# RWKV keys of a hybrid decoder layer: four keys first, products within the chunks one head pair later

## Chip, cores and metric

One core of one Trainium2 chip runs the whole program. The metric is device time in microseconds (us): 2528.46 us before the change, the median of three runs (2526.56, 2528.46, 2529.1).

## What is computed

One decoder layer on a sequence of 2048 tokens with 1024 channels. The input is normalised and modulated, projected once to all branches (RWKV-7, Mamba-2, gated linear attention), the branches are gated, merged and projected out. What the change touches is the RWKV branch, cut here to its keys and its recurrence:

```python
w = w0 + tanh(wd) @ w_up
decay = exp(-exp(-softplus(-w) - 0.5))
a = sigmoid(a0 + ad @ a_up)
kk = heads(k * k_k)
kk = kk / maximum(sqrt(sum(kk * kk, axis=-1, keepdims=True)), 1e-12)
k = k * (1 + (a - 1) * k_a)
# per token, state 64x64 per head:
sa = state @ -kk_t
state = state * w_t + sa * (kk_t * a_t) + v_t * k_t
y_t = state @ r_t
```

There are 8 heads of 64 channels. "The length of a key" below is the root of the sum of squares by which `kk` is divided.

## The kernel before

The sequence is worked in four quarters of 512 tokens (T). In each quarter, `mamba_gla` does the other two branches, then `rwkv` does this one, then 18 projections of merge logits follow (`gates_ahead` at the point "end"). After the last quarter `phase_o` does merging and output for all quarters.

A projection (`proj`, L322 to L332) makes one tile of 128 channels by 512 tokens with 24 matmuls (three for each of 8 slices of the input channels, weights and input split into a high and a low part), into one of two PSUM banks named mm. The weights come by DMA in halves of a tile, 512 columns each, and are split by ScalarE (L346) and VectorE (L347); `Weights` keeps three halves ahead in an order that `m_weights` and `r_weights` list in advance.

`rwkv` (L800) projects wd and ad, puts them through tanh and a split (L803 to L805), and then calls `rw_keys` (L829) for each of the four head pairs (two heads of 64 channels on 128 partitions). `rw_keys` for a head pair:

- makes decay and iclr logits with six matmuls on 64 rows each, three to bank pA from partitions 0 to 63 and three to pB from partitions 64 to 127 (L839), and from them the running decay G and its inverse GI (L841 to L848) and ta (L853);
- projects one tile of merge logits (`gates_ahead` at "r0" to "r3"), the key k (L855) and the receptance r (L867), each key and receptance mixed with its predecessor token by `rw_mix` (L822 to L825);
- finds the key's lengths: square (L858), a matmul with a block of ones (L860, to pA), Relu, Ln, Exp on ScalarE (L861 to L863);
- forms ar and bk, two tiles of 512 by 2 columns (L865 to L877, VectorE);
- makes the products within the chunks: for each of 8 chunks of 64 tokens and each of two heads one matmul bk times ar (L887), 64 rows by 128 columns, head 0 to bank pA and head 1 to bank pB, four chunks at a time, so that one head pair takes two passes over the same two banks; VectorE masks each bank into A (L890, four instructions for a head pair).

After the four head pairs, `rw_inverse` inverts 32x32 blocks of A on VectorE after a trip through DRAM (at a lower priority, offset INV), `rw_values` projects values and gates, `rw_merge` and `rw_chain` run the recurrence over 8 chunks.

The order on each engine is set when the program is built, by a scheduler that starts the ready instruction of highest priority. Priority is the order in the source; `later` moves work back (INV, POST, LATE) and, with the negative offset SOON, forward (the reads of the mm banks). On the chip each engine takes its instructions in that fixed order. Tiles of SBUF and PSUM are named by a tag that has a number of buffers: d, G, GI, ta, kn, r, sq, p2, cA, cB have one, k and y two, A eight, the PSUM banks pA, pB, pC, pE one and pD two.

Of the kernel before, what the change touches and what calls it, by code (L numbers as in the profile page):

```python
# [9 lines left out]
AF = mybir.ActivationFunctionType  # L10
ALU = mybir.AluOpType
# [3 lines left out]
P = 128  # L15
SEQ = 2048
D = 1024
T = 512
# [4 lines left out]
NCH = T // CH  # L23
NU = 4
# [69 lines left out]
def sb(g, tag, shape, dt=F32):  # L94
    n, bufs = SBUF_TAGS[tag]
    size = 1
    for x in shape[1:]:
        size *= x
    assert size <= n, (tag, shape)
    t = g.sp.tile([P, n], dt, name=tag, tag=tag, bufs=bufs)[0:shape[0], 0:size]  # L100
    if len(shape) == 3:
        t = t.rearrange("p (a b) -> p a b", a=shape[1])
    elif len(shape) == 4:
        t = t.rearrange("p (a b c) -> p a b c", a=shape[1], b=shape[2])
    return t


def small(g, tag, shape, bufs=2):
    return g.sp.tile(list(shape), F32, name=tag, tag=tag, bufs=bufs)


def pt(g, tag, shape=(P, T)):
    t = g.pp.tile([P, T], F32, name=tag, tag=tag, bufs=PSUM_TAGS[tag])
    size = 1
    for x in shape[1:]:
        size *= x
    t = t[0:shape[0], 0:size]
    if len(shape) == 3:
        t = t.rearrange("p (a b) -> p a b", a=shape[1])
    elif len(shape) == 4:  # L120
        t = t.rearrange("p (a b c) -> p a b c", a=shape[1], b=shape[2])
    return t


@contextmanager
def later(g, n):

    with g.tc.high_priority(-n):
        yield
# [188 lines left out]
def wtile(g, key):  # L318
    return g.A["w_pair"] if key == "dtgk" else g.A["w_in"][TILES[key]]
# [25 lines left out]
def split2(g, src, hi, lo):  # L345
    g.nc.scalar.copy(hi, src)  # L346
    g.nc.vector.tensor_tensor(lo, src, hi, ALU.subtract)  # L347
# [59 lines left out]
def mproj(g, hT):  # L407
    ps = pt(g, "mm")
    proj(g, ps, hT)
    return ps  # L410
# [328 lines left out]
def gate_keys(g, q, point):  # L739
    n = AHEAD.get(point, 0)  # L740
    at = g.planned[q]
    g.planned[q] += n
    return [("lg", b * 8 + i) for b, i in GATES[at:at + n]]


def gates_ahead(g, m, q, point):

    nc = g.nc
    for _ in range(AHEAD.get(point, 0)):
        ps = mproj(g, m.hT)  # L750
        t = sb(g, "th", [P, T])
        with later(g, SOON):
            nc.scalar.activation(t, ps, AF.Tanh, scale=0.5)  # L753
        nc.sync.dma_start(g.gates_dram[q, g.gated[q]], t)
        g.gated[q] += 1
# [1 line left out]


def r_weights(g, q):
    keys = ["wdad"]  # L760
    for pts in ((("k", "k"), ("r", "r")), (("v", "v"), ("g", "rg"))):
        for hp in range(NU):
            for point, key in pts:
                keys += gate_keys(g, q, ("r", point + str(hp))) + [(key, hp)]
    keys += gate_keys(g, q, ("r", "end"))
    return [wtile(g, key) for key in keys]
# [33 lines left out]
def rwkv(g, m, q):  # L800
    nc = g.nc
    wm = rw_mix(g, m, 12, "ysq")
    nc.scalar.activation(wm[0:64], wm[0:64], AF.Tanh)  # L803
    m.wm = sb(g, "wm", [P, T], F32R), sb(g, "wn", [P, T], F32R)
    split2(g, wm, *m.wm)  # L805
    hps = [rw_keys(g, m, q, i, str(i)) for i in range(NU)]
    with later(g, INV):
        rw_inverse(g, m, q, hps)
    for i, h in enumerate(hps):
        rw_values(g, m, q, i, h, str(i))  # L810
    rw_merge(g, m, hps)
    rw_chain(g, m, q, hps)


def rw_mix(g, m, i, tag):

    nc = g.nc
    ps = mproj(g, m.hT)
    o = sb(g, tag, [P, T])
    mu = g.v("mu", i)  # L820
    with later(g, SOON):
        nc.scalar.activation(o, ps, AF.Copy, scale=m.mu1[:, i:i + 1])  # L822
        nc.vector.scalar_tensor_tensor(o[:, 1:T], ps[:, 0:T - 1], mu, o[:, 1:T], ALU.mult, ALU.add)
        nc.vector.scalar_tensor_tensor(o[:, 0:1], m.prev[:, i:i + 1], mu, o[:, 0:1], ALU.mult, ALU.add)
        nc.vector.tensor_copy(m.prev[:, i:i + 1], ps[:, T - 1:T])  # L825
    return o


def rw_keys(g, m, q, hp, at):  # L829

    nc = g.nc
    h = Ctx()
    cb = lambda t: t.rearrange("p (c t) -> p c t", c=NCH)
    col = lambda t: t[:, hp:hp + 1]

    pw, pa = pt(g, "pA"), pt(g, "pB")
    for n, (a, b) in enumerate(((0, 0), (0, 1), (1, 0))):
        for o, js in ((pw, slice(0, 64)), (pa, slice(64, 128))):
            nc.tensor.matmul(o, m.up[a][js, hp * P:(hp + 1) * P], m.wm[b][js], start=n == 0, stop=n == 2)  # L839
    cs = sb(g, "d", [P, T])  # L840
    nc.scalar.activation(cs, pw, AF.Tanh, scale=0.5, bias=col(m.w0h))  # L841
    nc.vector.tensor_scalar(cs, cs, 1.0, None, ALU.add)
    nc.vector.tensor_tensor_scan(cs, g.scan[0], cs, 0.0, ALU.mult, ALU.add)
    G = sb(g, "G", [P, NCH, CH + 1])
    nc.gpsimd.memset(G[:, :, 0:1], 1.0)
    nc.scalar.activation(G[:, :, 1:], cb(cs), AF.Exp, scale=-0.5 * RW_C)
    GI = sb(g, "GI", [P, T])
    nc.scalar.activation(GI, cs, AF.Exp, scale=0.5 * RW_C)  # L848
    h.gc = small(g, "gc", [P, NCH], 4)
    nc.vector.tensor_copy(h.gc, G[:, :, CH])  # L850

    ta = sb(g, "ta", [P, T])
    nc.scalar.activation(ta, pa, AF.Tanh, scale=0.5, bias=col(m.a0h))  # L853
    gates_ahead(g, m, q, ("r", "k" + at))
    k = rw_mix(g, m, 4 + hp, ("k", "k", "y", "y")[hp])  # L855

    sq = sb(g, "sq", [P, T])
    nc.scalar.activation(sq, k, AF.Square, scale=g.v("k_k", hp))  # L858
    pn = pt(g, "pA")
    nc.tensor.matmul(pn, g.c("bones", P), sq, start=True, stop=True)  # L860
    nc.scalar.activation(sq, pn, AF.Relu, bias=g.c("m24"))  # L861
    nc.scalar.activation(sq, sq, AF.Ln, scale=65536.0, bias=g.c("epskk"))
    nc.scalar.activation(sq, sq, AF.Exp, scale=-0.5, bias=g.c("expkk"))  # L863
    kn = sb(g, "kn", [P, T])
    nc.vector.scalar_tensor_tensor(kn, k, g.v("k_k", hp), sq, ALU.mult, ALU.mult)  # L865
    gates_ahead(g, m, q, ("r", "r" + at))
    r = rw_mix(g, m, hp, "r")  # L867
    h.ar = sb(g, "ar", [P, NCH, 2, CH])
    h.bk = sb(g, "bk", [P, NCH, 2, CH])
    nc.vector.tensor_tensor(h.ar[:, :, 1], cb(r), G[:, :, 1:], ALU.mult)  # L870
    nc.vector.tensor_tensor(h.ar[:, :, 0], cb(kn), G[:, :, 0:CH], ALU.mult)
    nc.vector.scalar_tensor_tensor(kn, ta, 1.0, kn, ALU.add, ALU.mult)
    nc.vector.scalar_tensor_tensor(h.bk[:, :, 0], cb(kn), -0.5, cb(GI), ALU.mult, ALU.mult)
    nc.vector.tensor_scalar(ta, ta, col(m.kah), col(m.kab), ALU.mult, ALU.add)
    nc.vector.tensor_tensor(k, k, ta, ALU.mult)
    nc.vector.tensor_tensor(h.bk[:, :, 1], cb(k), cb(GI), ALU.mult)  # L876
    nc.vector.scalar_tensor_tensor(k, r, col(m.rkh), k, ALU.mult, ALU.mult)  # L877
    h.rk = k

    h.A = [sb(g, "A", [P, NCH, P]) for _ in range(2)]  # L880
    for c4 in range(0, NCH, 4):
        p = [pt(g, tag, [P, 4, P]) for tag in ("pA", "pB")]
        for i in range(4):
            c = c4 + i
            for j in range(2):
                js = slice(64 * j, 64 * j + 64)
                nc.tensor.matmul(p[j][:, i], h.bk[js, c].rearrange("p x t -> p (x t)"),  # L887
                                 h.ar[js, c].rearrange("p x t -> p (x t)"), start=True, stop=True)
        for j in range(2):
            nc.vector.tensor_tensor(h.A[j][:, c4:c4 + 4], p[j],  # L890
                                    g.c("gmask", P)[:, None, :].to_broadcast([P, 4, P]), ALU.mult)
    return h


def rw_values(g, m, q, hp, h, at):

    nc = g.nc
    gates_ahead(g, m, q, ("r", "v" + at))
    h.v = rw_mix(g, m, 8 + hp, "v")
    pb = pt(g, "pA")  # L900
    nc.tensor.matmul(pb, g.c("bones", P), h.rk, start=True, stop=True)
    p2 = sb(g, "p2", [P, T])
    nc.vector.tensor_tensor(p2, pb, h.v, ALU.mult)
    gates_ahead(g, m, q, ("r", "g" + at))
    pg = mproj(g, m.hT)
    th = sb(g, "th", [P, T])
    nc.scalar.activation(th, pg, AF.Tanh, scale=0.5)
    sg = sb(g, "sgo", [P, T])
    nc.vector.scalar_tensor_tensor(sg, th, 1.0, pg, ALU.add, ALU.mult)
    nc.vector.scalar_tensor_tensor(p2, p2, m.lnb[:, hp:hp + 1], sg, ALU.add, ALU.mult)  # L910
    nc.sync.dma_start(m.sd[q * NU + hp, 0], sg)
    nc.sync.dma_start(m.sd[q * NU + hp, 1], p2)
# [381 lines left out]
```

## Time and profile before

| what | value |
|---|---|
| median of three runs | 2528.46 us |
| the profiled execution, its own time | 2527.74 us |
| its span in the profile | 2526.0 us |
| TensorE (PE) busy | 2439.9 us, 97% |
| VectorE (DVE) busy | 1629.8 us, 65% |
| ScalarE (ACT) busy | 1236.1 us, 49% |

Busy time counts each engine's own instructions; a matmul's end is modelled and overlaps its successor, so for TensorE the distance between starts tells more than the duration. "PEclk" is the clock granted to TensorE as a share of 2.4 GHz; 0.5 is 1.2 GHz. A wait is idle time of an engine, put down to the instruction that ended it.

### The profile page before, as it was taken

The numbers are of one execution on the slowest core, as the hardware profiler recorded it, in microseconds if no ns is written. First come the engines' busy times: TensorE is split into PE (matmuls) and PEld (weight loads), VectorE is DVE, ScalarE is ACT, GpSimd is POOL, SyncE is SP. The second block draws the span as 40 slices with busy tenths as digits, with TensorE's granted clock in tenths as the row PEclk, the third lists the DMA queues.
The fourth block names the chain that finished last, engine by engine and source line by source line (L and its number), as shares of the span: only waits on it lengthen the run. The fifth ranks groups of instructions, "written<-read, shape, count | busy, mean of one in ns | idle before, by whom it ended". The sixth has DMA issues, their size and how long they took to land.

```text
span 2526.0 us, 39561 instructions
## 1 busy us (share of the span) xinstructions
PE 2439.9 (97%) x14756; PEld 1905.2 (75%) x14756; DVE 1629.8 (65%) x3180; ACT 1236.1 (49%) x2073; POOL 22.0 (1%) x68
## 2 busy tenths in 40 slices
PE   6999999999999999999999999999999999999998
PEld 4777777777777777777777777777777778787876
DVE  7694666546945664559566645694666547778696
ACT  4465643555656435556564355565643544233333
POOL 0000000000000000000000000000000000000000
PEclk9999999999999999999999999999999999999999
DMA  8322344343322442533234434322346367476571
GB/s 284 124 95 92 98 129 135 102 156 114 100 92 86 121 149 92 168 113 101 92 95 127 142 105 152 113 96 97 97 133 191 100 209 244 163 237 208 200 254 59
DMA packets 256916, 345.19 MB, mean 137 GB/s; under 512 B 63394, under 2 KB 112690, under 8 KB 256724
## 3 DMA queue, kind: packets, MB, share of 16 engines
q1 hardware_dynamic: 256724, 342.67, 42.2%
q8 instruction: 116, 1.90, 0.3%
q14 instruction: 76, 0.62, 0.1%
HBM read 275.40 MB, written 67.18 MB: 136 GB/s over the span
## 4 chain that ended last, share of the span: by engine, by line
PE 72%; DVE 12%; ACT 9%; issue 4%; DMA 3%; SPq 0%; DVEq 0%; ACTq 0%
PE mm L331 13%; PE mm L332 13%; PE mm L330 13%; PE mm L1153 3%; PE mm L1154 3%; PE mm L1155 3%; DVE wl L347 2%; DVE iU L939 1%; DVE iX L937 1%; PE pA L887 1%; ACT wh L346 1%; DMA wr<-in_w_in 1%; ACT L863 1%; PE pD L589 1%; PE pC L1044 1%
## 5 line engine op out<-in xcount | busy, mean ns | idle before, releaser
L330 PE MATMUL mm<-hTh,wh 128*128 128x512 f32 x2080 | 837.4, 403 | 4.5 <-ACT wh L346 3.1
L332 PE MATMUL mm<-hTh,wl 128*128 128x512 f32 x2080 | 836.3, 402 | 1.0 <-DVE wl L347 1.0
L331 PE MATMUL mm<-hTl,wh 128*128 128x512 f32 x2080 | 832.7, 400 | 0.0
L346 ACT CAST wh<-wr 128x512 fp32r<-128x512 f32 (+1 forms) x676 | 413.8, 618 | 778.6 <-PE mm L331 514.4
L347 DVE TENSOR_TENSOR wl<-wr,wh 128x512 fp32r<-128x512 f32 x672 | 458.3, 688 | 406.8 <-ACT wh L346 363.8
L330 PEld LDWEIGHTS mm<-hTh,wh 128*128 128x128 f32 x2080 | 393.9, 189 | 98.2 <-issue 9.8
L331 PEld LDWEIGHTS mm<-hTl,wh 128*128 128x128 f32 x2080 | 393.8, 189 | 91.7 <-issue 10.6
L332 PEld LDWEIGHTS mm<-hTh,wl 128*128 128x128 f32 x2080 | 393.7, 189 | 89.4 <-issue 7.4
L1153 PE MATMUL mm<-hTh,wh 128*128 128x512 f32 x256 | 100.1, 391 | 6.6 <-DVE th L1207 5.2
L1155 PE MATMUL mm<-hTh,wl 128*128 128x512 f32 x256 | 99.7, 390 | 0.0
L1154 PE MATMUL mm<-hTl,wh 128*128 128x512 f32 x256 | 99.7, 389 | 0.0
L753 ACT ACTIVATE th<-mm 128x512 f32<-128x512 f32 x96 | 57.0, 594 | 15.9 <-DMA gatesd<-th 7.7
L1153 PEld LDWEIGHTS mm<-hTh,wh 128*128 128x128 f32 x256 | 48.0, 188 | 18.6 <-issue 7.2
L1155 PEld LDWEIGHTS mm<-hTh,wl 128*128 128x128 f32 x256 | 48.1, 188 | 10.1
L1154 PEld LDWEIGHTS mm<-hTl,wh 128*128 128x128 f32 x256 | 48.1, 188 | 10.0
L887 PE MATMUL pA<-ar,bk 64*128 64x128 f32 x256 | 40.5, 291 | 13.6 <-DVE bk L876 13.6
L887 PEld LDWEIGHTS pA<-ar,bk 64*128 64x128 f32 x256 | 32.0, 187 | 26.1 <-DVE bk L876 20.3
L1154 PE MATMUL mm<-A,wh 128*128 128x512 f32 x128 | 50.8, 396 | 0.0
L1155 PE MATMUL mm<-A,wl 128*128 128x512 f32 x128 | 50.7, 396 | 0.0
L1153 PE MATMUL mm<-A,wh 128*128 128x512 f32 x128 | 50.7, 396 | 0.0
L937 DVE TENSOR_TENSOR iX<-iU,iN 128x31 f32<-128x31 f32 (+15 forms) x124 | 42.4, 342 | 3.4
L939 DVE TENSOR_TENSOR iU<-iU,iX 128x31 f32<-128x31 f32 (+15 forms) x124 | 42.3, 341 | 3.0
(712 smaller groups left out, 3664.7 us busy)
## 6 DMA issues: line engine op xcount, KB each, us to landing
wr<-in_w_in SPq DMA_DIRECT2D x520, 256.0 KB
gatesd<-th SPq DMA_DIRECT2D x96, 256.0 KB
wr<-in_w_branch SPq DMA_DIRECT2D x96, 256.0 KB
wr<-in_w_out SPq DMA_DIRECT2D x56, 256.0 KB
k<-gatesd SPq DMA_DIRECT2D x48, 256.0 KB
A<-in_x SPq DMA_DIRECT2D x16, 512.0 KB
A<-in_ada_w SPq DMA_DIRECT2D x16, 512.0 KB
y<-acsd SPq DMA_DIRECT2D x32, 256.0 KB
```

What stands on the lines that cost most here:

```text
L330: nc.tensor.matmul(ps, a, hh[k], start=k == 0, stop=False)
L331: nc.tensor.matmul(ps, a, hl[k], start=False, stop=False)
L332: nc.tensor.matmul(ps, b, hh[k], start=False, stop=k == KD - 1)
L346: g.nc.scalar.copy(hi, src)
L347: g.nc.vector.tensor_tensor(lo, src, hi, ALU.subtract)
L753: nc.scalar.activation(t, ps, AF.Tanh, scale=0.5)
L887: nc.tensor.matmul(p[j][:, i], h.bk[js, c].rearrange("p x t -> p (x t)"), h.ar[js, c].rearrange("p x t -> p (x t)"), start=True, stop=True)
L937: nc.vector.tensor_tensor(x, U[:, 0:a, t:t + 1].to_broadcast([nl, a, b]), N[:, t:t + 1, t + 1:].to_broadcast([nl, a, b]), ALU.mult)
L939: nc.vector.tensor_tensor(U[:, 0:a, t + 1:], U[:, 0:a, t + 1:], x, ALU.add)
L1153: nc.tensor.matmul(pb, a, yh, start=k == 0, stop=False)
L1154: nc.tensor.matmul(pb, a, yl, start=False, stop=False)
L1155: nc.tensor.matmul(pb, l, yh, start=False, stop=k == 3)
```

## The change

All four keys of a quarter are projected first, in a new function `rw_norm_keys`, which also finds their lengths: squares and sums key by key, then Ln for all four and Exp for all four. `rw_keys` takes key and inverse length from it and no longer makes the products within the chunks. These are in a new function `rw_within`, called for a head pair after `rw_keys` of the next one; it uses four banks (pA, pB, pC, pE) at once, so that the two passes become one. The decay and iclr logits go to the two buffers of pD instead of pA and pB, the key sums to pD instead of pA. Inside `rw_keys` the receptance and its two uses move behind the work on the key. The weight list follows. The inverse lengths sit in sq, p2, cA and cB.

```diff
 def r_weights(g, q):
-    keys = ["wdad"]
-    for pts in ((("k", "k"), ("r", "r")), (("v", "v"), ("g", "rg"))):
+    keys = ["wdad"] + [("k", hp) for hp in range(NU)]
+    for pts in ((("r", "r"),), (("v", "v"), ("g", "rg"))):
...
-    hps = [rw_keys(g, m, q, i, str(i)) for i in range(NU)]
+    ks = rw_norm_keys(g, m)
+    hps = []
+    for i, k in enumerate(ks):
+        hps.append(rw_keys(g, m, q, i, k, str(i)))
+        if i:
+            rw_within(g, hps[i - 1])
+    rw_within(g, hps[-1])
...
+def rw_norm_keys(g, m):
+    nc = g.nc
+    ks = []
+    for hp in range(NU):
+        k = rw_mix(g, m, 4 + hp, ("k", "k", "y", "y")[hp])
+        sq = sb(g, ("sq", "p2", "cA", "cB")[hp], [P, T])
+        nc.scalar.activation(sq, k, AF.Square, scale=g.v("k_k", hp))
+        pn = pt(g, "pD")
+        nc.tensor.matmul(pn, g.c("bones", P), sq, start=True, stop=True)
+        nc.scalar.activation(sq, pn, AF.Relu, bias=g.c("m24"))
+        ks.append((k, sq))
+    for k, sq in ks:
+        nc.scalar.activation(sq, sq, AF.Ln, scale=65536.0, bias=g.c("epskk"))
+    for k, sq in ks:
+        nc.scalar.activation(sq, sq, AF.Exp, scale=-0.5, bias=g.c("expkk"))
+    return ks
...
-    pw, pa = pt(g, "pA"), pt(g, "pB")
+    pw, pa = pt(g, "pD"), pt(g, "pD")
...
-    gates_ahead(g, m, q, ("r", "k" + at))
-    k = rw_mix(g, m, 4 + hp, ("k", "k", "y", "y")[hp])
-
-    sq = sb(g, "sq", [P, T])
-    nc.scalar.activation(sq, k, AF.Square, scale=g.v("k_k", hp))
-    pn = pt(g, "pA")
-    nc.tensor.matmul(pn, g.c("bones", P), sq, start=True, stop=True)
-    nc.scalar.activation(sq, pn, AF.Relu, bias=g.c("m24"))
-    nc.scalar.activation(sq, sq, AF.Ln, scale=65536.0, bias=g.c("epskk"))
-    nc.scalar.activation(sq, sq, AF.Exp, scale=-0.5, bias=g.c("expkk"))
     kn = sb(g, "kn", [P, T])
-    nc.vector.scalar_tensor_tensor(kn, k, g.v("k_k", hp), sq, ALU.mult, ALU.mult)
-    gates_ahead(g, m, q, ("r", "r" + at))
-    r = rw_mix(g, m, hp, "r")
+    nc.vector.scalar_tensor_tensor(kn, k, g.v("k_k", hp), inv, ALU.mult, ALU.mult)
     h.ar = sb(g, "ar", [P, NCH, 2, CH])
     h.bk = sb(g, "bk", [P, NCH, 2, CH])
-    nc.vector.tensor_tensor(h.ar[:, :, 1], cb(r), G[:, :, 1:], ALU.mult)
     nc.vector.tensor_tensor(h.ar[:, :, 0], cb(kn), G[:, :, 0:CH], ALU.mult)
...
     nc.vector.tensor_tensor(h.bk[:, :, 1], cb(k), cb(GI), ALU.mult)
+    gates_ahead(g, m, q, ("r", "r" + at))
+    r = rw_mix(g, m, hp, "r")
+    nc.vector.tensor_tensor(h.ar[:, :, 1], cb(r), G[:, :, 1:], ALU.mult)
     nc.vector.scalar_tensor_tensor(k, r, col(m.rkh), k, ALU.mult, ALU.mult)
     h.rk = k
-
+    return h
+
+
+def rw_within(g, h):
+    nc = g.nc
     h.A = [sb(g, "A", [P, NCH, P]) for _ in range(2)]
-    for c4 in range(0, NCH, 4):
-        p = [pt(g, tag, [P, 4, P]) for tag in ("pA", "pB")]
-        for i in range(4):
-            c = c4 + i
-            for j in range(2):
-                js = slice(64 * j, 64 * j + 64)
-                nc.tensor.matmul(p[j][:, i], h.bk[js, c].rearrange("p x t -> p (x t)"),
-                                 h.ar[js, c].rearrange("p x t -> p (x t)"), start=True, stop=True)
+    p = [[pt(g, tag, [P, 4, P]) for tag in tags] for tags in (("pA", "pB"), ("pC", "pE"))]
+    for c in range(NCH):
         for j in range(2):
-            nc.vector.tensor_tensor(h.A[j][:, c4:c4 + 4], p[j],
+            js = slice(64 * j, 64 * j + 64)
+            nc.tensor.matmul(p[c // 4][j][:, c % 4], h.bk[js, c].rearrange("p x t -> p (x t)"),
+                             h.ar[js, c].rearrange("p x t -> p (x t)"), start=True, stop=True)
+    for i in range(2):
+        for j in range(2):
+            nc.vector.tensor_tensor(h.A[j][:, 4 * i:4 * i + 4], p[i][j],
                                     g.c("gmask", P)[:, None, :].to_broadcast([P, 4, P]), ALU.mult)
-    return h
```

## Rows read from the trace of the kernel before

**Rows 1.** The page: its first line and part 1.

```profile
span 2526.0 us, 39561 instructions
...
PE 2439.9 (97%) x14756; PEld 1905.2 (75%) x14756; DVE 1629.8 (65%) x3180; ACT 1236.1 (49%) x2073; POOL 22.0 (1%) x68
```

**Rows 2.** Waits of PE, whole span: us in total, times, longest us.

```profile
PE pA L887 <- DVE bk L876: 13.6, 16, 1.2
...
PE pA L839 <- ACT wm L346: 6.5, 4, 1.6
...
PE pA L389 <- ACT r L391: 2.3, 3, 1.1
```

**Rows 3.** Timeline of PE, third head pair, first quarter: start, us, engine, line.

```profile
310.85 0.37 PE L887 MATMUL pA<-ar,bk 64*128 64x128 f32 x1 [0.88 <-DVE bk L876]
310.85 0.37 PE L887 MATMUL pB<-ar,bk 64*128 64x128 f32 x1
...
311.94 0.50 PE L330 MATMUL mm<-hTh,wh 128*128 128x512 f32 x1
...
312.83 0.82 PE L887 MATMUL pA<-ar,bk 64*128 64x128 f32 x5
...
314.46 0.50 PE L330 MATMUL mm<-hTh,wh 128*128 128x512 f32 x1
...
315.36 0.51 PE L839 MATMUL pA<-wm,up 64*128 64x512 f32 x1
...
316.59 0.50 PE L330 MATMUL mm<-hTh,wh 128*128 128x512 f32 x1
...
318.56 1.02 PE L860 MATMUL pA<-sq,cs 128*128 128x512 f32 x2
...
319.64 0.40 PE L330 MATMUL mm<-hTh,wh 128*128 128x512 f32 x1
...
321.01 0.39 PE L330 MATMUL mm<-hTh,wh 128*128 128x512 f32 x1
...
326.45 0.39 PE L330 MATMUL mm<-hTh,wh 128*128 128x512 f32 x1
```

**Rows 4.** Timeline of PE where the first quarter's keys begin.

```profile
260.34 0.39 PE L330 MATMUL mm<-hTh,wh 128*128 128x512 f32 x1
262.35 0.49 PE L839 MATMUL pA<-wm,up 64*128 64x512 f32 x1 [1.62 <-ACT wm L346]
262.35 0.49 PE L839 MATMUL pB<-wm,up 64*128 64x512 f32 x1
262.77 0.51 PE L331 MATMUL mm<-hTl,wh 128*128 128x512 f32 x1
```

**Rows 5.** Windows: PE, PEld, DVE, ACT, POOL busy (x), PEclk, DMA share, GB/s.

```profile
770.00:778.00 8.00, 8.00 (x20) 4.89 (x21) 5.60 (x10) 7.33 (x11) 0.00 (x0) 0.58 0.24 81
...
1774.00:1782.00 8.00, 8.00 (x20) 4.94 (x19) 5.43 (x10) 7.16 (x11) 0.00 (x0) 0.57 0.22 72
```

**Rows 6.** Groups of instructions, ACT, whole span: busy us, mean ns, idle before.

```profile
L862 ACT ACT_TABLE_LOAD x16 | 20.5, 1283 | 0.3
```

**Rows 7.** Window of one head pair, from products to products; columns as in rows 5.

```profile
310.80:333.60 22.80, 22.12 (x113) 17.11 (x113) 15.49 (x29) 12.81 (x19) 0.30 (x2) 1.00 0.43 122
```

**Rows 8.** Groups of DVE in that window: busy us, mean ns, idle before.

```profile
L347 DVE TENSOR_TENSOR wl<-wr,wh 128x512 fp32r<-128x512 f32 x7 | 4.8, 688 | 1.7 <-DMA gatesd<-th 1.4 <-ACT wh L346 0.2
L890 DVE TENSOR_TENSOR A<-pA,cs 128x512 f32<-128x512 f32 x2 | 1.4, 691 | 1.0 <-PE pA L887 1.0
...
L823 DVE SCALAR_TENSOR_TENSOR y<-mm,vec,y 128x511 f32<-128x511 f32 x1 | 0.7, 746 | 0.0
```

**Rows 9.** First quarter: the chain's last state steps, the merge logits' last reads (first, last start).

```profile
L1061 DVE TENSOR_TENSOR rs<-rs,gcu x7: 417/426/428, 457.5 to 501.3; 128x256 f32<-128x256 f32 x7
...
L753 ACT ACTIVATE th<-mm x18: 580/591/600, 404.4 to 560.7; 128x512 f32<-128x512 f32 x18
```

More of the change, by code (lines that the diff above doesn't have):

```diff
@@ L826, in rw_mix, with rw_keys @@
     return o
-def rw_keys(g, m, q, hp, at):
+def rw_norm_keys(g, m):
[14 more added lines that the diff above has]
+    return ks
+def rw_keys(g, m, q, hp, ks, at):
     nc = g.nc
     h = Ctx()
+    k, inv = ks
     cb = lambda t: t.rearrange("p (c t) -> p c t", c=NCH)
     col = lambda t: t[:, hp:hp + 1]
-    pw, pa = pt(g, "pA"), pt(g, "pB")
+    pw, pa = pt(g, "pD"), pt(g, "pD")
     for n, (a, b) in enumerate(((0, 0), (0, 1), (1, 0))):
```

## The prediction

> **What bounds the kernel now.** I read part 1 of the page first. TensorE (PE) is busy 2439.9 of 2526.0 us [rows 1], in a program whose projections follow each other without a gap, so a microsecond comes off the end only if PE works shorter or idles less. The second view is the list of PE's waits [rows 2]. The largest belongs to the part that is changed: all 16 groups of products within the chunks (L887, four head pairs in four quarters) wait for bk of their own head pair, 13.6 us in all. Another, 6.5 us in four waits, is that of the decay logits (L839) for the split of wd and ad at the start of each quarter's keys. The third view is PE's timeline, because idle time is not all that is lost there [rows 3]. The first 16 products of a head pair run two at a time on the two halves of the rows (two start at 310.85) and take 310.85 to 311.94, 1.09 us. The second 16 take 312.83 to 314.46, 1.63 us: five on pA go first and alone, because pB was planned to come free later.
>
> **Does PE time carry to the end?** In the first quarter the last step of the recurrence starts at 501.3 us, while the last projection of merge logits is read at 560.7 us [rows 9]. So 59 us of projections that depend on nothing in the branch still lie behind the chain. A saving among the keys moves both earlier, and the chain may even come some us later without PE running dry.
>
> **The change part by part.**
>
> 1. *Products one head pair later.* Products of pair i now stand behind the receptance of pair i+1; bk and ar of pair i are then complete. 12 of the 16 waits lose their cause. The fourth pair has no successor: its products follow the third's, and what fills the time is the projection of the first value, as now. I leave these four at the mean of 0.85 us (13.6/16). Gain 13.6 - 3.4 = 10.2 us; bounds 0 and 13.6.
>
> 2. *Four banks, one pass.* The second 16 products at the first's speed, without their lead-in: 0.88 instead of 1.63 us (1.09 less about 0.2 for the first pair; an estimate from rows 3), and one change between projection and product fewer, about 0.1 us (such a first matmul comes 0.33 instead of 0.23 us after its predecessor: an estimate from the same timeline). 0.85 x 16 = 13.6 us. Bounds: 0, if the order breaks the group up again, and 16 x 1.0.
>
> 3. *Start of a quarter's keys.* Now PE starts the first key at 260.34, then stands until 262.35 for wm [rows 4], because the logits come first in the order. Afterwards four keys, 4 x 24 matmuls at 0.227 us (5.44 us from 321.01 to 326.45 for 24 [rows 3]), stand ahead of the logits, 21.8 us in which wd and ad are long split. Gain 6.5 us [rows 2]; bounds 5 and 6.5.
>
> 4. *The clock behind that wait.* In the second and the fourth quarter, in the 8 us after that wait, PE was granted 0.58 and 0.57 of its clock [rows 5], that is, 1.2 GHz for most of the stretch; the engine had stood still just before. 8 x 0.42 + 8 x 0.43 = 6.8 us of PE's work lost. With nothing to wait for, I take all of it; bounds 0 (some other small stall does the same) and 6.8.
>
> 5. *Logits in pD.* The six matmuls of a later pair take 315.36 to 316.59, 1.23 us [rows 3], partly one by one because pB came free late. Two at once take 262.35 to 262.77, 0.42 us with the change to the next kind [rows 4]. Three such pairs: 0.42 + 2 x 0.23 = 0.88. Gain 0.35 x 12 = 4.2 us (the first pair of a quarter is mostly paired already); bounds 0 and 0.35 x 16 = 5.6. Their banks are read by two tanh, with nothing of VectorE in between.
>
> 6. *Table loads.* Ln and Exp each load a table for every key, 16 + 16 loads of 1.283 us (L862, and as many on L863) [rows 6]. Batched they are 8, and 31 us of ScalarE go. ScalarE is busy 49% [rows 1] and none of PE's waits that are left hangs on it, so I cost them at nothing; if the scheduler runs a Ln early because ScalarE is free, some loads come back, also for nothing. The key sums (L860) cost the same in pD: 318.56 to 319.64 less one matmul, 0.85 us.
>
> 7. *What is new.* Squares wait for p2 and cB, which the branch before uses last; k of pairs 2 and 3 waits for y to be written out; key sums share pD with the logits. No row shows these waits. Nearest is the wait of a matmul for a ScalarE read, up to 1.1 us (L389) [rows 2]. Bounds 0 and two such per quarter, 8.8; I take 1 us a quarter, 4 us. The SP queue issues as many DMAs as before, weights merely in another order; the DMAs of A for pairs 0 to 2 leave one pair later, but the inverse needs the fourth's too, and that comes where it came before. POOL's memset of G only follows the pair, as now.
>
> Sum: -10.2 - 13.6 - 6.5 - 6.8 - 4.2 + 4 = -37.3. The profiled execution took 2527.74 us (span 2526.0 plus 1.7 around it), 0.7 below the median. 2527.7 - 37.3 = 2490.4; set against the median, 2491 us.
>
> **VectorE, the nearest next bound.** Between two pairs PE now takes 22.80 us and VectorE is busy 15.49 of them, 68% [rows 7]. With keys gone from it, a pair's stretch on PE is 22.80 - 0.88 - 0.85 - 0.35 - 5.44 - 0.85 = 14.4 us. VectorE loses one mixing of k (0.75 at least) and about three weight splits (7 are in the window, 4 belong to the two projections that stay; 3 x 0.69) [rows 8]: 12.7 us, 88%. It fits, but with 1.7 us of air. The row behind: the four maskings of a pair take 4 x 0.69 = 2.8 us [rows 8], while 32 products in one pass would take about 2 us. The Trainium skill speaks against the change here: TensorEngine Tiling (Array Packing), section PSUM Bottleneck, warns that packing the array speeds up TensorE but not the emptying of PSUM, which may become the bottleneck. Worked as a mechanism of this kernel it is the second rival; by it the sum would be a loss, by the rows a gain; no row of before shows PSUM's emptying as what ends a stretch.
>
> **The rivals.**
>
> *A. Only the waits go.* The scheduler mixes products with projections, or frees banks unevenly, and neither products nor logits pack: parts 1, 3, 4 and 7 remain, -10.2 - 6.5 - 6.8 + 4 = -19.5, about 2509 us. For it: the scheduler did break up the second 16. Against: four banks that have been free for a whole pair give it no reason. Chance 0.13.
>
> *B. VectorE bounds the pairs (slower).* G, GI, d, ta and kn have one buffer each, so each pair's decay waits until the pair before has made ar, and VectorE also waits for ScalarE in that loop. If it stays filled no better than now, 12.7 / 0.68 = 18.7 us a pair, 4.3 more than PE's 14.4: 16 x 4.3 = 69 us against a gain of 37, about 2560 us. It turns the sign from 37.3 / 16 = 2.3 us more a pair, at a fill under 12.7 / 16.7 = 76%. Against: its present idle time is there because PE is slower, not because the loop is full. Chance 0.06.
>
> *C. Not later after all.* The scheduler's plan sets products as early as it thinks bk is ready; it has been about 0.9 us too early 16 times. If it pulls them ahead of the receptance in the same way, waits stay and passes stay broken: parts 3, 4, 5, 7, -6.5 - 6.8 - 4.2 + 4 = -13.5, about 2515 us. Against: the receptance has the higher priority and is always ready. Chance 0.07.
>
> *D. No difference.* New small waits and another half-clock stretch eat what is won. Chance 0.05.
>
> **How the numbers follow.** The forecast's own case has 0.69, and spans 2478 (all upper bounds and no new wait: -48.5, about 2480, and a little for the estimates) to 2502. 0.2% of the time, 5 us, is about what a measurement can tell from no change. Faster: forecast, A and C, 0.89; same: D, 0.05; slower: B, 0.06. The range takes in the forecast and A, with the estimates' error: 2476 to 2512.
>
> **What would show it.** In the changed kernel's waits, the products' line should show about four waits instead of 16, and the wait for wm should be gone; in PE's timeline, 32 products in about 2 us and six logits in under 0.9; the granted clock near 1.00 where the second and fourth quarters' keys begin; 8 loads, not 32, for Ln and Exp; from a quarter's first key to its last products about 9 us less. If VectorE is over 90% busy between pairs and PE waits for ar, bk or a mm bank, B is right and the forecast wrong.

## The result and the profile after

The changed kernel takes 2539.67 us (2533.62 to 2549.93), the one before beside it 2529.1 us (2526.56 to 2531.9): a ratio of 1.0053, 95% interval 1.0035 to 1.0071. (The ratios here are those on record; the quotient of the two medians is 1.0042.) It is slower by about half a per cent, where 2491 us and a gain were forecast. The profiled execution took 2540.58 us, with a span of 2538.8 us.

The page of the kernel after, its first line and part 1, answers to [rows 1]:

```profile
span 2538.8 us, 39623 instructions
...
PE 2438.0 (96%) x14756; PEld 1906.4 (75%) x14756; DVE 1628.5 (64%) x3180; ACT 1234.1 (49%) x2073; POOL 28.2 (1%) x68
```

ScalarE is as busy as before: the 31 us of table loads have not gone. Waits of PE after (us in total, times, longest us), for [rows 2]:

```profile
PE pD L844 <- ACT cA L842: 18.2, 4, 4.6
...
PE pE L354 <- ACT SV L346: 6.1, 5, 1.5
PE pA L907 <- DVE ar L892: 5.9, 4, 1.7
...
PE pD L844 <- ACT cB L842: 4.7, 4, 1.6
...
PE pD L844 <- ACT sq L842: 4.2, 4, 1.1
```

What was to go did go: four waits for products instead of 16, none for wm. In their place stand 12 waits of the key sums (L844) for ScalarE's squares, 18.2 + 4.7 + 4.2 = 27.1 us, and four waits of 1.46 us at the start of each quarter's keys for SV, a split of the branch before (L354). In the kernel before that line reads:

```profile
PE pE L354 <- ACT SV L346: 0.2, 1, 0.2
```

PE's timeline (start, us) for [rows 3]: the third key's sum, a later pair's products and logits, and the last pair's products:

```profile
285.30 0.39 PE L330 MATMUL mm<-hTh,wh 128*128 128x512 f32 x1
...
290.22 1.55 PE L844 MATMUL pD<-cA,cs 128*128 128x512 f32 x2 [4.54 <-ACT cA L842]
...
322.67 0.37 PE L907 MATMUL pA<-ar,bk 64*128 64x128 f32 x1
...
324.45 0.27 PE L907 MATMUL pE<-ar,bk 64*128 64x128 f32 x1
324.47 0.48 PE L865 MATMUL pD<-wm,up 64*128 64x512 f32 x2
...
336.47 0.37 PE L907 MATMUL pA<-ar,bk 64*128 64x128 f32 x1
...
353.75 1.13 PE L907 MATMUL pA<-ar,bk 64*128 64x128 f32 x8 [1.42 <-DVE ar L892]
354.81 0.50 PE L330 MATMUL mm<-hTh,wh 128*128 128x512 f32 x1
355.24 1.09 PE L907 MATMUL pB<-ar,bk 64*128 64x128 f32 x5
...
358.60 0.79 PE L331 MATMUL mm<-hTl,wh 128*128 128x512 f32 x1
```

The third sum waits 4.54 us. 32 products take one pass of 1.80 us (322.67 to 324.47), and a pair's stretch is 13.80 us long (to 336.47). The fourth pair's products follow directly behind the third's: they wait for ar, break up into eight on pA alone and a projection's matmul between, and end 4.85 us after they began (5.02, 5.18 and 3.46 us in the other quarters).

Four windows of the kernel after (columns as in rows 5): the keys of the first quarter, the half clock among them, one pair, the last pair's products.

```profile
265.60:305.00 39.40, 31.33 (x116) 21.78 (x115) 13.74 (x27) 34.09 (x46) 0.00 (x0) 0.96 0.21 74
290.80:294.20 3.40, 3.40 (x9) 2.31 (x8) 0.60 (x1) 2.36 (x3) 0.00 (x0) 0.50 0.21 77
322.70:336.50 13.80, 13.80 (x89) 11.20 (x88) 12.97 (x25) 5.76 (x11) 0.69 (x2) 1.00 0.43 118
355.60:362.40 6.80, 6.80 (x33) 5.80 (x32) 3.04 (x5) 0.00 (x0) 0.00 (x0) 0.50 0.39 82
```

Among the keys ScalarE is busy 34.09 of 39.4 us, 87%, and PE 80%. In the whole program they have 49% and 96%; in this stretch the order of the two is turned round.

### The profile page after: what moved, and what is told of

Same layout as the page of the kernel before. It is cut to its first block, busy times and chain, and to the rows that moved or that the text cites. A ratio compares the mean times of both kernels' runs of the same rounds, so it can differ in the third digit from the quotient of the medians.

```text
span 2538.8 us, 39623 instructions
## 1 busy us (share of the span) xinstructions
PE 2438.0 (96%) x14756; PEld 1906.4 (75%) x14756; DVE 1628.5 (64%) x3180; ACT 1234.1 (49%) x2073; POOL 28.2 (1%) x68
## 4 chain that ended last, share of the span: by engine, by line
PE 77%; ACT 9%; DVE 7%; DMA 3%; issue 3%; SPq 0%; ACTq 0%; DVEq 0%
PE mm L330 15%; PE mm L331 15%; PE mm L332 15%; PE mm L1173 3%; PE mm L1175 3%; PE mm L1174 3%; DVE wl L347 1%; ACT wh L346 1%; PE pC L1064 1%; PE pD L589 1%; PE pD L585 1%; DVE iU L959 1%; PE pE L1067 1%; PE pC L1047 1%; PE pD L844 1%
## 5 line engine op out<-in xcount | busy, mean ns | idle before, releaser
L521 DVE SCALAR_TENSOR_TENSOR ar<-G,cwh,ar 128x512 f32<-128x512 f32 x48 | 35.9, 749 | 3.9 <-ACT ar L517 3.3
L521 DVE SCALAR_TENSOR_TENSOR bk<-G,cwh,bk 128x512 f32<-128x512 f32 x48 | 35.7, 745 | 2.9 <-ACT bk L517 2.7
```

The lines of the kernel that those rows point to most:

```text
L521: nc.vector.scalar_tensor_tensor(o, R[:, j:j + T], m.cw[:, j * 8 + i:j * 8 + i + 1], o, ALU.mult, ALU.add)
```

## Where the time went: two theories

ScalarE's groups in the keys' stretch of the kernel after (busy us, mean ns, idle before): the loads ahead of Ln and of Exp.

```profile
L848 ACT ACT_TABLE_LOAD x4 | 5.1, 1283 | 0.1
L850 ACT ACT_TABLE_LOAD x3 | 3.8, 1283 | 0.1
```

ScalarE's timeline in the same stretch (start, us):

```profile
278.13 1.28 ACT L848 ACT_TABLE_LOAD   x1
279.42 0.72 ACT L848 ACTIVATE sq<-sq,cs 128x512 f32<-128x512 f32 x1
280.16 1.28 ACT L850 ACT_TABLE_LOAD   x1
281.46 0.72 ACT L850 ACTIVATE sq<-sq,cs 128x512 f32<-128x512 f32 x1
...
283.28 1.28 ACT L848 ACT_TABLE_LOAD   x1
...
285.32 1.28 ACT L850 ACT_TABLE_LOAD   x1
286.62 0.72 ACT L850 ACTIVATE p<-p,cs 128x512 f32<-128x512 f32 x1
...
287.75 0.68 ACT L828 ACTIVATE y<-mm,mu 128x512 f32<-128x512 f32 x1
...
289.45 0.72 ACT L842 ACTIVATE cA<-y,vec 128x512 f32<-128x512 f32 x1 [1.02 <-DVE y L830]
```

Ln (L848) and Exp (L850) of the first two keys run before the third key is mixed (L828, 287.75) and squared (L842, 289.45). PE, whose order is fixed, has projected for the third key since 285.30 and stands at its sum for 4.54 us, until 290.22 (PE's timeline above).

**Theory M1.** The scheduler starts each Ln and Exp as soon as its sum is there, so loads come key by key, and they stand in ScalarE's queue ahead of the next key's mixing and square. Per key ScalarE then has 0.69 (mixing) + 0.72 (square) + 0.69 (Relu) + 0.72 (Ln) + 0.72 (Exp) + 2.57 (two loads) + 1.2 (two casts of weights) = 7.3 us, where PE has 5.46 (projection) + 0.85 (sum) = 6.3 us.

**Theory M2.** The fourth pair's products directly behind the third's cost more than their wait: the half clock behind them (6.8 us in each of the first three quarters) and the broken packing. VectorE's timeline there names what they meet: ar is formed from 352.92 on, and the third pair's banks pB to pE are masked only behind it, though PE had filled them by 352.3.

```profile
352.92 0.68 DVE L892 TENSOR_TENSOR ar<-r,G 128x512 f32<-128x512 f32 x1
...
354.19 0.68 DVE L911 TENSOR_TENSOR A<-pB,cs 128x512 f32<-128x512 f32 x1
...
355.38 0.68 DVE L911 TENSOR_TENSOR A<-pE,cs 128x512 f32<-128x512 f32 x1
```

The fourth pair's products reach pB at 355.24 and pE at 356.76, one bank after the other behind these maskings.

**Rivals.** VectorE, 94% busy in a pair's stretch, is the bound (B); or the product half of the change carries the loss, and the keys do not; or the key sums simply stand too close behind their key on PE, whatever ScalarE does. In the expectations on record M1 is called theory 1, the last rival theory 2 and M2 theory 3.

## The experiments

**No table loads.** The lengths are not computed here: Ln becomes Tanh, which needed no load next to Exp here. ScalarE has 32 instructions fewer, all of them loads; PE's order in the trace is the same but for 8 of 14756 places, and on ScalarE and VectorE a few instructions change places.

```diff
-        nc.scalar.activation(sq, sq, AF.Ln, scale=65536.0, bias=g.c("epskk"))
+        nc.scalar.activation(sq, sq, AF.Tanh, scale=65536.0, bias=g.c("epskk"))
...
-        nc.scalar.activation(sq, sq, AF.Exp, scale=-0.5, bias=g.c("expkk"))
+        nc.scalar.activation(sq, sq, AF.Exp, scale=-9.6, bias=g.c("expkk"))
```

> The changed kernel with Ln of the key lengths replaced by tanh, which shares a table with Exp (and another scale in Exp so that the numbers stay small): no table is loaded for the lengths, the order on TensorE is the same to the last instruction. Lengths are not computed here. Theory 1 (ScalarE's queue: Ln and Exp run key by key with two table loads each, the mixing and squaring of later keys stand behind them, and TensorE, in its fixed order, waits at the key sums): the waits of the key sums L844 fall from 27.1 us to under 12, about 15 us of waits and 5 to 10 us of half clock go, 2515 to 2520 us against 2540 for the changed kernel. Theory 2 (the key sums simply stand too close behind their own key on TensorE, whatever ScalarE does): the waits stay over 20 us and the time within 5 us of 2540.

Measured: 2508.75 us, ratio 0.9917 (0.9889 to 0.9945) to the kernel before, less than the 2515 to 2520 us expected. PE's waits in this kernel:

```profile
PE pA L907 <- DVE ar L892: 5.6, 4, 1.4
...
PE pD L844 <- ACT sq L842: 4.3, 4, 1.1
```

Its window over the first quarter's keys:

```profile
264.30:299.00 34.70, 32.16 (x129) 23.23 (x128) 17.98 (x35) 27.50 (x45) 0.58 (x1) 1.00 0.28 91
```

Of 27.1 us of waits for squares 4.3 are left, the clock in the keys is 1.00, and 1.36% of the time is back, some 34 us (31 by the medians). M1 is shown; the rival that the sums stand too close to their key is out, and so is VectorE as the main bound: its work is the same. The last pair gains with it: its waits are as they were, 5.6 us, but the half clock behind them fell from 20.5 us in three quarters to 10.2 us in two.

**Batching enforced.** The biases of Ln are made to depend on the fourth sum and those of Exp on the last Ln, so that neither can start early.

```diff
+    e = small(g, "kfe", [P, 2], 1)
+    nc.vector.scalar_tensor_tensor(e[:, 0:1], ks[-1][1][:, 0:1], 0.0, g.c("epskk"), ALU.mult, ALU.add)
...
-        nc.scalar.activation(sq, sq, AF.Ln, scale=65536.0, bias=g.c("epskk"))
+        nc.scalar.activation(sq, sq, AF.Ln, scale=65536.0, bias=e[:, 0:1])
...
```

> The changed kernel with the batching enforced: the biases of the four Ln hang on the fourth key's sum and those of the four Exp on the last Ln, so that no Ln can start early; two small VectorE instructions more in a quarter. Theory 1: 8 table loads instead of 32 for the lengths, key-sum waits under 12 us, time 2512 to 2522 us. Theory 2: waits and time as in the changed kernel, 2535 to 2545. A third way it could go: the lump of Ln and Exp behind the fourth key delays the first pair's decay, and a new wait of several us appears at the first receptances: over 2525 with key-sum waits under 12.

Measured: 2546.64 us, ratio 1.0073 (1.0044 to 1.0101), slower still. PE's waits in this kernel:

```profile
PE pD L868 <- ACT ta L882: 9.6, 4, 2.4
PE pA L910 <- DVE ar L895: 9.6, 4, 2.6
...
PE pD L844 <- ACT sq L842: 4.2, 4, 1.1
```

ScalarE's timeline behind the fourth key:

```profile
294.40 1.28 ACT L850 ACT_TABLE_LOAD   x1
...
303.46 0.61 ACT L875 ACTIVATE G<-d 128x512 f32<-128x512 f32 x1
...
304.50 0.67 ACT L882 ACTIVATE ta<-pD,a0h 128x512 f32<-128x512 f32 x1
```

The key sums wait 4.2 us as without loads, which agrees with M1; but the eight activations now form one lump, and the first pair's decay and iclr (G at 303.46, ta at 304.50) stand behind it. PE waits 9.6 us there, at the second pair's logits, for ta; the other 9.6 us are the last pair's products waiting for ar, 5.9 us in the change as it is. In the stage measured below this kernel takes 561.0 us, 6 less than the change; what it loses lies behind the stage and was not traced to a cause. Even then the batch is not clean: a tanh of the merge logits came in among the four Ln and cost two loads, the one shown among them.

**Last pair later.** The fourth pair's products move behind the first value and gate.

```diff
+    rw_values(g, m, q, 0, hps[0], "0")
     rw_within(g, hps[-1])
...
-    for i, h in enumerate(hps):
+    for i, h in enumerate(hps[1:], 1):
```

> The changed kernel with the products of the fourth pair behind the first value and gate projections instead of directly behind the third pair's products. Theory 3 (part of the loss is at the last pair: products wait for ar, find their banks still being masked, and the clock falls to half behind it): the 5.9 us of waits at L907 go, the dips of the clock near the last products go, time about 2526 to 2532. If theory 1 is all of it: 2536 us or more.

Measured: 2528.61 us, ratio 1.0 (0.9979 to 1.002). No wait of the products is among the largest any more, and the key sums wait as they did, as PE's waits show:

```profile
PE pD L845 <- ACT cA L843: 18.3, 4, 4.6
```

From 1.0053 to 1.0 is 0.53%, 13 us (11 by the medians), for an edit that takes away four waits of 5.9 us together: M2 is shown, with more behind the wait than in it. The pass is whole again, 1.99 us in every quarter, and no half clock follows it.

**Products alone.** Each key goes back into its pair (one sum in pD); four banks, the later products and the logits in pD stay.

```diff
-    ks = rw_norm_keys(g, m)
...
+    k = rw_mix(g, m, 4 + hp, ("k", "k", "y", "y")[hp])
+    sq = sb(g, "sq", [P, T])
...
+    pn = pt(g, "pD")
+    nc.tensor.matmul(pn, g.c("bones", P), sq, start=True, stop=True)
...
```

> Only the second half of the change: products one pair later on four banks, logits and key sums in pD, but each key projected and its length found inside its own pair, as before. If the forecast's parts 1, 2 and 5 hold (waits of products, one pass, paired logits) and the keys-first part alone is what lost the time: 2529 - 10 - 14 - 4 = 2501, with the last pair's loss of some 10 us still in it 2505 to 2512. If deferring the products is what costs: 2529 or more.

Measured: 2538.9 us, ratio 1.0044 (1.0025 to 1.0064): a miss, no gain but a loss. PE's waits in the kernel with the products alone:

```profile
PE pD L863 <- ACT sq L861: 24.2, 12, 2.3
...
PE pD L844 <- ACT wm L346: 6.5, 4, 1.6
PE pA L894 <- DVE bk L876: 5.5, 4, 1.4
```

VectorE's timeline there, ahead of the third key's mixing, its last row:

```profile
310.95 0.68 DVE L898 TENSOR_TENSOR A<-pE,cs 128x512 f32<-128x512 f32 x1
...
312.48 1.22 DVE L848 TENSOR_TENSOR_SCAN d<-scan,d 128x512 f32<-128x512 f32 x1
...
314.80 0.75 DVE L828 SCALAR_TENSOR_TENSOR y<-mm,vec,y 128x511 f32<-128x511 f32 x1
```

PE's timeline at that key's sum:

```profile
316.55 1.12 PE L863 MATMUL pD<-sq,cs 128*128 128x512 f32 x2 [2.01 <-ACT sq L861]
```

With the wait for bk gone, PE arrives sooner at the next instruction that hangs on the key. Masks, scan and weight splits of VectorE lie ahead of the key's mixing (314.80), so the square is late, and 12 sums wait 24.2 us. That VectorE's order is the cause is read from the trace; the last experiment bears it out in part. The second half of the change alone moves the wait from the products to the sums. So the product half loses by itself too, for another reason than the keys do.

**Keys first alone.** Products directly behind their pair, in two passes over pA and pB, as before.

```diff
-        if i:
-            rw_within(g, hps[i - 1])
-    rw_within(g, hps[-1])
+        rw_within(g, hps[i])
...
```

> Only the first half of the change: four keys first, but the products right behind their own pair, in two passes over two banks; logits in pD. Theory 1: the key sums' waits stay at about 27 us, the products wait for ar of their own pair in all 16 places: 2535 us or more, slower than the kernel before. If the keys-first part is harmless and the loss comes from the deferred products: 2520 or less.

Measured: 2554.83 us, ratio 1.0119 (1.009 to 1.0148). The sums wait as in the whole change, and the products' waits come on top (PE's waits):

```profile
PE pD L842 <- ACT cA L840: 18.3, 4, 4.6
...
PE pA L906 <- DVE A L909: 6.0, 12, 1.0
```

**Both losses out.** The first and the third edit together; the lengths are again not computed.

> Tanh in place of Ln (lengths not computed, no table loads) and the last pair's products behind the first value and gate. If the two losses are separate and add up: 31 us (table loads in ScalarE's queue) and 11 us (last pair) under the changed kernel, about 2497 us. If the last pair's loss is only a consequence of ScalarE's lateness: about 2508, as with the loads alone away.

Measured: 2495.48 us, ratio 0.988 (0.9853 to 0.9908). From 1.0053 that is 1.73%, 44 us; 34 and 13 apart, so the two losses add up but for some 3 us (both edits take away half clock behind the last pair). Together they are the difference to the forecast, within 5 us by the medians and 7 by the ratio.

**Work between key and sum.** The whole computation, with loads: behind each key stands one projection of merge logits (four fewer at the end of the quarter), ahead of its sum, and the last pair's products move as above.

```diff
+        gates_ahead(g, m, q, ("r", "k" + str(hp)))
         pn = pt(g, "pD")
...
+    rw_values(g, m, q, 0, hps[0], "0")
     rw_within(g, hps[-1])
...
```

> Full computation. The changed kernel with one of the 18 last projections of merge logits behind each of the four keys, ahead of its key sum (4 there, 14 at the end), and the last pair's products behind the first value and gate. Theory 1 in its sharper form (in the keys' stretch ScalarE has some 7.3 us of work for a key, two table loads of 1.28 among it, against 6.3 us of TensorE): with 11.8 us of TensorE for a key ScalarE keeps up, the key sums do not wait (under 5 us), and the time is that of the kernel without loads, 2492 to 2505 us. Theory 2 (key sums too close to their key): gone as well, the same time, but then the loads would not have mattered. If the projections are missed at the end, behind the recurrence: 2510 or more.

Measured: 2503.77 us, ratio 0.9917 (0.9892 to 0.9943): faster than both kernels. PE's waits for squares are down to those of each quarter's first key:

```profile
PE pD L849 <- ACT sq L846: 4.2, 4, 1.1
```

The window of its keys, with the four projections in it:

```profile
265.20:316.00 50.80, 48.27 (x200) 36.77 (x199) 20.23 (x36) 40.45 (x57) 0.00 (x0) 1.00 0.33 114
```

ScalarE keeps its loads and its seven or so microseconds a key, but PE now has 11.8 us a key (6.3 + 5.46), 95% filled at full clock.

**The same in the product half.** Products alone, with the pair's own merge-logit projection moved between square and sum, and the last pair later.

> Full computation. Only the second half of the change (products one pair later, four banks), keys inside their pairs as before, but each key sum behind the pair's merge-logit projection instead of directly behind its key, and the last pair's products behind the first value and gate. If the 24 us of key-sum waits in the run with the second half alone came from TensorE reaching the sum before VectorE had mixed the key (VectorE masks the pair before at that time): the waits go, 2495 to 2508 us. If deferring the products costs in another way (half clock, banks): 2520 or more.

Measured: 2510.45 us, ratio 0.9935 (0.9915 to 0.9955), a little above what was expected, because only part of the waits went (PE's waits):

```profile
PE pD L865 <- ACT sq L862: 14.4, 8, 2.1
```

## Why the prediction was wrong

Measured as the stretch from the tanh of wd and ad to the quarter's last gate tanh, in us for the four quarters (worked out from ScalarE's timelines):

| kernel | quarters | sum | against before |
|---|---|---|---|
| before | 136.8, 139.8, 136.8, 139.7 | 553.1 | |
| after | 142.1, 142.6, 142.9, 139.5 | 567.1 | +14.0 |
| no loads | 132.8, 131.3, 134.4, 131.3 | 529.8 | -23.3 |
| last pair later | 136.5, 136.9, 136.9, 136.8 | 547.1 | -6.0 |
| both losses out | 128.7, 128.8, 128.7, 128.7 | 514.9 | -38.2 |

The prediction's sum was -37.3 us. With both losses out the stage gains 38.2; some 3 us of that only come from where the stage begins (633 or 634 matmuls in it before, 630 or 631 after). The whole program gains 33 (2528.59 to 2495.48), and 3 us of the rest are in a later wait for VectorE's y, 11.7 us against 8.4 before. So the gains were priced well in sum, and two losses were missing.

- *Part 6, table loads at nothing: the step that failed.* "ScalarE is busy 49%" is a share over the whole span. The change gathers four keys in 39 us, where ScalarE has 7.3 us a key against PE's 6.3. The text even allowed for the loads' coming back, "also for nothing"; they came back whole (8 a quarter: four for Ln, three for Exp, and one for the decay's tanh that came between the fourth Ln and its Exp), and ahead of the next key's square. Cost: 27.1 - 4.3 = 22.8 us of waits, and half clock with them (290.8 to 294.2, 792.6 to 799.4, 1301.1 to 1308 and 1809.7 to 1813.1 us, 20.5 us at 0.50; PE stood still in the waits for 4.9 of these, so 7.8 us of its work lost): 31 us. The run without loads gains 37 in the stage; of the 6 beyond these 31, 5 are half clock behind the last pair.
- *The skill on this.* The Trainium skill, ScalarE: Activation LUTs, section "Table sets: the hidden batching unit", tells to batch activations by table set, and says that Ln followed by Exp needs one load. Here the trace disagrees with the second: a load of 1283 ns stands before Ln and before Exp of each quarter's first three keys. For the first, the enforced batch was at 1.0073 no gain: the sums' waits went, others came, and why the program as a whole lost is open.
- *Part 7, new waits at 4 us.* The bounds were 0 and 8.8; it came to 27.1. The row taken as nearest was a wait for a ScalarE read of 1.1 us; a queue with loads in it had to be added up per key instead. Without loads the sums wait 4.3 us, a wait of 1.1 at each quarter's first key: that is the term's size without the queue. The wait for SV, 5.8 us, is a second new one that no part names.
- *Part 1, products later.* Right in count: four waits, 5.9 us against 3.4 forecast. Wrong in "as now": in the kernel before, the fourth pair's products had a pair's work between them and the third's; now they have only the third's products. What was priced at 3.4 us costs 13 (20 in the stage): half clock (355.6 to 362.4 and the like in the second and third quarters, 10.2 us lost) and a broken pass.
- *Part 2, four banks.* Right: 1.80 us, forecast about 2, but not for the last pair.
- *Part 3, the wait for wm.* Gone, but its 6.5 us were not won: every kernel here with the keys first waits 4 x 1.46 = 5.8 us for SV instead, whose split stands right behind wm's in ScalarE's queue (267.42 and 266.92 us), and those that keep the keys in their pairs wait 6.5 us for wm and not for SV.
- *Part 4, the half clock.* It went from the places named (1.00 in 770.4 to 778.4 and 1785.1 to 1793.1, where these quarters' keys begin now), and came back at the new waits: 18 us lost to it in seven places, where 6.8 were lost in two. The prediction's own bound 0 said so ("some other small stall does the same").
- *Part 5, logits in pD.* Right: six matmuls from 324.47 to about 325.25, 0.8 us.
- *Rival B, VectorE.* A pair's stretch is 13.80 us (forecast 14.4) with VectorE 94% busy (forecast 88%), and PE is busy throughout. It did not bind there, nor did emptying the four banks. At the last pair both did: its products come 1.7 us behind the third's, wait for ar in VectorE's queue and find the banks still being masked, four maskings of 0.68 us against a pass of 1.80. So the sign named for B came true at one place a quarter, as M2. In the product half alone, with the keys among the pairs, its order did delay the squares.

That the loss went through D's mechanism, new waits and another half clock, is right in kind, but it had a chance of 0.05 and "no difference" as its size. A slower result had only B, which happened at the last pair alone and cost 13 us there, not the 69 of its price.

Open: why the four merge-logit projections cost the 8 us by which the version with them stays behind the one without loads (2503.77 and 2495.48). Its stage takes 150.4 us a quarter with the four projections in it, 128.6 without their 21.8 (4 x 5.46), so they cost it elsewhere: between and behind the four stages PE's waits add up to 40.6 us, against 31.8 in the other kernel (idle times over 0.1 us, worked out from the traces). What moves them there was not tried.

## What to carry to other kernels

When work is gathered in one place, add up each engine's time per item there, loads included: a share over the whole span says nothing of a stretch. Grouping calls in the source does not group them on the chip when a scheduler starts whatever is ready, and a group enforced by a dependence delays the work behind it; independent work of the engine that waits, put between producer and consumer, was worth more here. A wait that is removed can come back at the next instruction in the same order that hangs on the same data or the same engine's queue (the sums for the products, SV for wm), so look for that one first.

## What was not expected of the hardware

The length of a wait alone does not say whether half clock follows it. Behind the 4.54 us at 290.22 PE was granted 0.50 for 3.4 us; behind a last pair whose wait was 1.42 us it was granted 0.50 for 6.8 us, with PE at products of 64 rows just before; in the run without loads the same wait of 1.41 us stands in all four quarters, and half clock followed in two of them (347.3 to 350.7 and 1340.5 to 1347.4 us); in the products-alone kernel a wait of 2.01 us left the clock at 1.00, as its window around it shows:

```profile
303.10:325.50 22.40, 20.39 (x113) 16.02 (x112) 15.98 (x31) 12.92 (x20) 0.30 (x2) 1.00 0.43 122
```

And VectorE, filled to 12.97 of 13.80 us, made PE wait nowhere in a pair's stretch; it did where the next products came without a stretch between.
